# Two PSUM copies of the recurrent head group on one engine, in a one-layer hybrid decoder step

## The chip, the cores and the metric

The kernel runs on one core of a Trainium2 chip. The metric is the device time of one execution in microseconds; the median of several runs is compared. One execution was also taken by the hardware profiler, and all rows quoted here are from it.

## The reference

One layer of a decoder for 256 new prompt tokens and 8 single decode tokens: a half-step SwiGLU FFN, a mixer in which 16 attention heads (sliding window of 128, four key/value heads) stand beside 16 RWKV-7 heads, a second half-step FFN, and a final RMSNorm. What the change touches is the recurrence of the RWKV-7 heads:

```python
def wkv_scan(S0, r, logw, k, v, kk, a):
    def step(S, inp):
        r_t, lw_t, k_t, v_t, kk_t, a_t = inp
        sa = jnp.einsum('bhij,bhj->bhi', S, -kk_t)
        S = (S * jnp.exp(lw_t)[:, :, None, :] + sa[..., None] * (kk_t * a_t)[:, :, None, :]
             + v_t[..., None] * k_t[:, :, None, :])
        return S, jnp.einsum('bhij,bhj->bhi', S, r_t)
```

and the layer around it:

```python
def trunk_layer(x, attend, shift0, wkv0, lp):
    x = x + FFN_RES * swiglu(rmsnorm(x, n1), f1g, f1u, f1d)
    proj = rmsnorm(x, nm) @ w_in
    o_att, k_buf, v_buf = attend(q, k, v, sinks)
    o_rwkv, shift, S = rwkv_time_mix(proj[..., ATT_COLS:], shift0, wkv0, ...)
    x = x + jnp.concatenate([o_att, o_rwkv], axis=-1) @ w_out
    x = x + FFN_RES * swiglu(rmsnorm(x, n2), f2g, f2u, f2d)
```

The model width is 2048, the FFN width 5504, a head is 64 wide. All values are float32.

## The kernel before

All 264 tokens are columns of one activation tile of 128 x 264 per 128 features. Each weight chunk of 128 x 512 is loaded by SyncE (`raw`), rounded by ScalarE to `hi` (L127), and the rest `lo` = `raw` - `hi` is made by VectorE or GpSimd (L128, through the helper at L58). A gemm step multiplies `hi` and `lo` with the two parts of the activations, three matmuls for each 128 rows (`mm`, L74). Four buffers each of `hi` and `lo` and six of `raw` are in flight. Three PSUM banks (`acc`) serve the gemms, five (`m`, given out by `mp()`) everything else.

The execution goes through the first FFN, the mixer's input projection (`win`; its weights are loaded from 753.6 to 1088.4 us), the mixer's output projection (`wout`, loaded from 1089.8 to 1222.3 us), and the second FFN. The recurrence is not run token by token: the 256 prompt tokens are cut into four chunks of 64, and within a chunk the recurrence is solved with small triangular matrices. The work of the 16 RWKV heads is written as Python generators, which are advanced one step (`tick`) after each gemm step, so that their small instructions lie among the gemm's. `prep` treats a pair of heads, `chain` a batch of two pairs; there are four batches (`BATCH`), and the preps of the next batch stand among the steps of the chain before.

In `chain`, VectorE first inverts 32 x 32 blocks in 30 dependent steps (`st`, `Xt`, L573 and L574), through scratch in DRAM on both sides. Then come, in order:

- matmuls of the inverse `TT` with the chunk's keys (`pW`) and with its values (`pU`), L634. `pU` is one PSUM bank; the matmuls put the two heads of a pair into opposite halves of the partitions.
- L637: ScalarE copies `pW` to `W`. L638: VectorE copies one half of `pU` (64 x 512) into the tile `uv`. L639: ScalarE copies the other half into the same tile.
- matmuls `pP` (from `BT` and `W`) and `pG` (from `gm` and `W`), L647 and L650; ScalarE copies `pP` to `PT` (L653), VectorE adds `pG` to `KR` (L655).
- matmuls `pN` (L662) and `pY` (L668), which read `uv`; VectorE makes `N` from `pN` (L670).
- three steps over the chunks: `PT` and `KR` with the state, L679 and L683 (`m<-N,PT` in the profile), and VectorE's updates `Z` and `S`.

The copies of `prep` that lie beside these on ScalarE are those of the transposed keys (`kr`, L516) and of `BT` (L523, L525).

The order on each engine is not written out: a planner lays all instructions out on its own model of the engines' times, takes the earlier instruction of the program where several are ready, and gives out the buffers and PSUM banks in that order. Instructions under `high_priority` and `keep_in_program_order` are excepted. It sets all semaphores too, and keeps two accesses to one PSUM bank by different engines apart. On the chip each engine works through its list in order.

Of the kernel before, what the change touches and what calls it, by code (L numbers as in the profile page):

```python
# [24 lines left out]
HALF = (slice(0, 64), slice(64, 128))  # L25
# [22 lines left out]
def body(tc, I, O):  # L48
    nc = tc.nc
    V, A, G, TE, SP = nc.vector, nc.scalar, nc.gpsimd, nc.tensor, nc.sync  # L50
# [44 lines left out]
    with ExitStack() as ctx:  # L95
# [17 lines left out]
        def mp():  # L113
            return pp.tile([P, 512], F32, tag="m", bufs=NM, name=uid("m"))
# [243 lines left out]
        def mixing_body(mx, n2, n3, XD):  # L358
# [3 lines left out]
            def ring(shape, tag, bufs):  # L362
                return mx.tile(list(shape), F32, tag=tag, bufs=bufs, name=uid(tag))
# [186 lines left out]
            def chain(bt):  # L550
# [18 lines left out]
                for s in range(1, 31):  # L569
                    m, w = -(-s // ng), 31 - s  # L570
                    t = ring((ng * nr, m, w), "st", 2)
# [24 lines left out]
                def quads(k):  # L596
                    return slice(k * 4, k * 4 + 4), slice(k * P, k * P + P)
# [9 lines left out]
                for k in range(n):  # L607
                    c, x = quads(k)
# [9 lines left out]
                for k in range(n):  # L618
                    c, x = quads(k)
# [4 lines left out]
                uv = bt.UV  # L624
                W, PT = ring((P, n, 3, 64), "W", 1), ring((P, n, 3, 64), "PT", 1)
                N = ring((P, n, 4, 64), "N", 1)
                pW, pU = mp(), mp()
# [7 lines left out]
                                       bt.KR[k][HALF[h], a, c, :])  # L635
                pW, pU = (ps.rearrange("p (k c t) -> p k c t", k=n, c=4) for ps in (pW, pU))
                A.copy(W, pW[:, :, 1:4, :])  # L637
                V.tensor_copy(uv[HALF[0], :, :, HALF[0]].rearrange("p c k t -> p k c t"), pU[HALF[1]])  # L638
                A.copy(uv[HALF[1], :, :, HALF[1]].rearrange("p c k t -> p k c t"), pU[HALF[0]])  # L639
                yield  # L640
                pP, pG = mp(), mp()
                for k in range(n):
# [62 lines left out]
                for k in range(n):  # L705
                    p, o = bt.p0 + k, Ys[k]
# [169 lines left out]
            for kind, i in SEQ:  # L876
                if kind == "b":
                    bt = newbatch(i)
                    for k in range(BATCH[i]):
                        p = bt.p0 + k  # L880
                        x = [shifted(2 + 3 * p + j, tmp()) for j in range(3)]
                        spawn(prep(p, bt, k, *x))
                    bat.append(spawn(chain(bt)))
                    bts.append(bt)
                    if len(bat) == len(BATCH):
                        A.dma_start(O["sh"], shc)
                elif kind == "kv":
                    w, p = i // 2, i % 2
# [6 lines left out]
                else:  # L895
# [6 lines left out]
                    if i % 4 == 3:  # L902
                        p = i // 4
# [188 lines left out]
```

## Time and profile before

| | |
|---|---|
| median of 3 runs | 2003.16 us (2001.62 to 2003.61) |
| the profiled execution | 2001.57 us, span 1999.8 us |
| mean granted TensorE clock | 0.997 |
| TensorE matmuls | busy 1969.5 us, 17212 instructions |
| VectorE | busy 1301.4 us, 2546 instructions |
| ScalarE | busy 1065.4 us, 2137 instructions |
| GpSimd | busy 343.1 us, 437 instructions |
| L638, VectorE | 4 copies of 64 x 512, 0.69 us each |
| L639, ScalarE | 4 copies of 64 x 512, 0.58 us each |

PE is TensorE's matmuls, PEld its weight loads, DVE VectorE, ACT ScalarE, POOL GpSimd, SP SyncE. In a row of the timeline stand the start and the duration in us, the engine, the line, the operation with its output and inputs, and in brackets how long the engine was idle before it and who released it. Pool tiles are named by their tag: `m` is one of the five small PSUM banks, `acc` one of the three of the gemms.

### The profile page before, as it was taken

How to read it: one execution, taken by the hardware profiler on the slowest of the kernel's cores; microseconds unless marked ns; L12 is line 12 of the kernel's file. 1: busy time of each engine (PE TensorE's matmuls, PEld its weight loads, DVE VectorE, ACT ScalarE, POOL GpSimd, SP SyncE). 2: the span in 40 equal slices, each digit the busy share in tenths (PEclk: the TensorE clock that was granted, in tenths of full speed). 3: DMA queues.
4: the chain of work that ended last, by engine and by line, in shares of the span. 5: the costliest groups of instructions: out<-in, count | busy, mean ns of one | idle time of the engine just before them, and what ended most of it. 6: DMA issues, size and time to landing. Idle time of an engine off the chain costs nothing.

```text
span 1999.8 us, 45897 instructions
## 1 busy us (share of the span) xinstructions
PE 1969.5 (98%) x17212; PEld 1933.6 (97%) x17212; DVE 1301.4 (65%) x2546; ACT 1065.4 (53%) x2137; POOL 343.1 (17%) x437
## 2 busy tenths in 40 slices
PE   9999999999999999998998999999999999999998
PEld 9999999999999999997987899999999999999997
DVE  5865555655556577687867676765666666666665
ACT  5644444444444456775666765654444444444445
POOL 0401001010010121121124553120101001010012
PEclk9999999999999999999999999999999999999999
DMA  7666666655556667554555546565666666666654
GB/s 230 178 190 194 185 192 191 184 184 176 187 178 184 181 196 222 160 148 121 155 144 148 162 144 196 174 181 178 187 190 192 181 190 194 184 192 183 195 179 146
DMA packets 229232, 358.77 MB, mean 179 GB/s; under 512 B 42616, under 2 KB 84240, under 8 KB 229008
## 3 DMA queue, kind: packets, MB, share of 16 engines
q1 hardware_dynamic: 223120, 349.72, 57.9%
q10 hardware_dynamic: 5888, 6.11, 1.0%
q8 instruction: 135, 2.21, 0.4%
q14 instruction: 89, 0.73, 0.1%
HBM read 347.59 MB, written 10.22 MB: 179 GB/s over the span
## 4 chain that ended last, share of the span: by engine, by line
PE 91%; DVE 4%; DMA 2%; ACT 1%; issue 1%; SPq 1%; POOL 0%; ACTq 0%; DVEq 0%; POOLq 0%
PE acc L74 84%; PE m L74 6%; DVE lo L58 1%; DMA raw<-in_gu 1%; DVE st L58 1%; DVE Xt L58 1%; DMA raw<-in_win 0%; ACT t L68 0%; ACT hi L127 0%; DMA sb<-Xt 0%; DMA TT<-sb 0%; DVE y L58 0%; SPq L562 0%; DMA Xt<-sa 0%; SPq L563 0%
## 5 line engine op out<-in xcount | busy, mean ns | idle before, releaser
L127 ACT CAST hi<-raw 128x512 fp32r<-128x512 f32 (+2 forms) x1304 | 778.5, 601 | 818.0 <-PE acc L74 725.1
L58 DVE TENSOR_TENSOR lo<-raw,hi 128x512 fp32r<-128x512 f32 (+1 forms) x1248 | 854.4, 688 | 535.8 <-ACT hi L127 512.0
L74 PE MATMUL acc<-s,hi 128*128 128x264 f32 x5940 | 1111.7, 286 | 1.1 <-ACT hi L127 1.1
L74 PEld LDWEIGHTS acc<-s,hi 128*128 128x128 f32 x5940 | 923.3, 188 | 8.4 <-ACT hi L127 1.8
L74 PE MATMUL acc<-s,lo 128*128 128x264 f32 x2970 | 848.2, 286 | 4.9 <-DVE lo L58 4.6
L74 PEld LDWEIGHTS acc<-s,lo 128*128 128x128 f32 x2970 | 558.4, 188 | 9.5 <-DVE lo L58 6.4
L74 PE MATMUL acc<-t,hi 128*128 128x264 f32 x2752 | 502.8, 284 | 0.0
L74 PEld LDWEIGHTS acc<-t,hi 128*128 128x128 f32 x2752 | 425.9, 188 | 0.0
L74 PE MATMUL acc<-t,lo 128*128 128x264 f32 x1376 | 388.5, 284 | 0.0
L58 POOL TENSOR_TENSOR t<-t,t 128x264 f32<-128x264 f32 (+1 forms) x148 | 150.8, 1019 | 1148.6 <-ACT hi L127 789.9
L74 PEld LDWEIGHTS acc<-t,lo 128*128 128x128 f32 x1376 | 258.1, 188 | 0.1
L74 PE MATMUL acc<-y,hi 128*128 128x264 f32 x648 | 123.9, 284 | 0.0
L74 PEld LDWEIGHTS acc<-y,hi 128*128 128x128 f32 x648 | 101.2, 188 | 0.2
L74 PE MATMUL acc<-y,lo 128*128 128x264 f32 x324 | 91.3, 282 | 0.0
L58 DVE TENSOR_TENSOR t<-acc,t 128x264 f32<-128x264 f32 x156 | 67.4, 432 | 35.9 <-PE acc L74 35.7
L58 POOL TENSOR_TENSOR lo<-raw,hi 128x512 fp32r<-128x512 f32 x56 | 75.4, 1347 | 63.3 <-ACT hi L127 36.9
L58 POOL TENSOR_TENSOR o<-o,o 128x264 f32<-128x264 f32 x43 | 36.5, 848 | 187.4 <-ACT o L68 181.7
L74 PE MATMUL acc<-o,hi 128*128 128x264 f32 x324 | 62.4, 282 | 0.0
L74 PEld LDWEIGHTS acc<-y,lo 128*128 128x128 f32 x324 | 60.9, 188 | 0.0
L61 DVE SCALAR_TENSOR_TENSOR s<-acc,s 128x264 f32<-128x264 f32 x96 | 40.6, 428 | 15.9 <-PE acc L74 15.5
L74 PEld LDWEIGHTS acc<-o,hi 128*128 128x128 f32 x324 | 50.0, 188 | 0.0
L74 PE MATMUL m<-s,hi 128*128 128x264 f32 x260 | 48.1, 285 | 0.0
(252 smaller groups left out, 1336.9 us busy)
## 6 DMA issues: line engine op xcount, KB each, us to landing
raw<-in_gu SPq DMA_DIRECT2D x688, 256.0 KB, 3.4
raw<-in_dn SPq DMA_DIRECT2D x224, 256.0 KB, 2.9
raw<-in_win SPq DMA_DIRECT2D x152, 256.0 KB, 3.5
raw<-in_dn SPq DMA_DIRECT2D x160, 192.0 KB, 2.7
raw<-in_wout SPq DMA_DIRECT2D x48, 256.0 KB, 3.3
raw<-in_wout SPq DMA_DIRECT2D x32, 128.0 KB, 3.1
s<-xsp SPq DMA_DIRECT2D x16, 132.0 KB, 3.9
ld<-in_sT SPq DMA_DIRECT2D x16, 128.0 KB, 3.6
```

Of the source, the lines that this page charges most:

```text
L58: return e.tensor_tensor(out=out, in0=a, in1=b, op=op)
L61: return V.scalar_tensor_tensor(out=out, in0=a, scalar=s, in1=b, op0=op0, op1=op1)
L74: TE.matmul(out, lhsT, rhs, start=start, stop=stop, **k)
L127: A.copy(hi[:, :w], raw[:, :w])
```

## The change

Both halves of `pU` are copied into `uv` by ScalarE, in a loop over the two halves, the former VectorE half first. Nothing else is edited; the planner lays out the whole program anew.

```diff
                 A.copy(W, pW[:, :, 1:4, :])
-                V.tensor_copy(uv[HALF[0], :, :, HALF[0]].rearrange("p c k t -> p k c t"), pU[HALF[1]])
-                A.copy(uv[HALF[1], :, :, HALF[1]].rearrange("p c k t -> p k c t"), pU[HALF[0]])
+                for h in range(2):
+                    A.copy(uv[HALF[h], :, :, HALF[h]].rearrange("p c k t -> p k c t"), pU[HALF[1 - h]])
                 yield
```

## The prediction

> **What bounds the kernel now.** I read the page's engine line and chain first, then the rows of the two lines that the diff touches, then the stretches around their four executions.
>
> ```profile
> PE 1969.5 (98%) x17212; PEld 1933.6 (97%) x17212; DVE 1301.4 (65%) x2546; ACT 1065.4 (53%) x2137; POOL 343.1 (17%) x437
> PE 91%; DVE 4%; DMA 2%; ACT 1%; issue 1%; SPq 1%; POOL 0%; ACTq 0%; DVEq 0%; POOLq 0%
> ...
> L638 DVE COPY uv<-m x4: 692/694/694, 924.3 to 1134.1; 64x512 f32<-64x512 f32 x4
> L639 ACT COPY uv<-m x4: 577/578/579, 925.0 to 1135.5; 64x512 f32<-64x512 f32 x4
>   PEld m L74: 2.4, 2
>   PE m L74: 2.2, 2
> ```
>
> TensorE is busy for 98% of the span, so an edit on other engines is worth only what it takes out of TensorE's few waits, or out of stretches in which TensorE's clock is low. The diff touches four pairs of copies, one for each batch of heads, at 924, 996, 1055 and 1134 us. The last two lines are the waits of weight loads and matmuls for L639: TensorE stood 2.2 us for it, in two places. The windows show the first one as the odd one out (the last two rows are of batch 2):
>
> ```profile
> 924.00:925.00 1.00, 0.00 (x0) 0.00 (x0) 0.95 (x3) 0.01 (x1) 0.00 (x0) 0.65 0.18 68
> 925.00:931.00 6.00, 5.38 (x101) 5.14 (x102) 5.49 (x25) 3.09 (x8) 0.10 (x1) 0.50 0.18 44
> 931.00:932.00 1.00, 1.00 (x9) 1.00 (x9) 0.42 (x3) 0.62 (x2) 0.21 (x2) 0.93 0.06 16
> ...
> 1052.00:1056.00 4.00, 1.76 (x55) 1.34 (x53) 3.83 (x15) 3.17 (x9) 3.61 (x3) 1.00 0.61 181
> 1058.00:1063.00 5.00, 2.65 (x36) 2.33 (x33) 4.69 (x19) 0.62 (x1) 1.65 (x3) 1.00 0.66 209
> ```
>
> Columns: stretch and length, busy us of PE, PEld, DVE, ACT, POOL, then the granted clock, DMA share, GB/s. Around batch 0 the clock falls to 0.50 for over 6 us; VectorE is nearly full (5.49 of 6.00), ScalarE half empty.
>
> **Batch 0, step by step.** ScalarE's, VectorE's and TensorE's rows (start, duration, idle before and its releaser in brackets):
>
> ```profile
> 921.59 0.48 ACT L637 COPY W<-m 128x384 f32<-128x384 f32 x1
> 921.96 1.08 ACT L516 COPY kr<-m 64x128 f32<-64x128 f32 x4
> 923.06 0.37 ACT L523 COPY BT<-m 128x256 f32<-128x256 f32 x1
> 923.45 0.37 ACT L525 COPY BT<-m 64x256 f32<-64x256 f32 x1
> 924.99 0.58 ACT L639 COPY uv<-m 64x512 f32<-64x512 f32 x1 [1.18 <-DVE uv L638]
> 925.47 0.36 ACT L525 COPY BT<-m 64x256 f32<-64x256 f32 x1
> ...
> 924.02 0.22 DVE L58 TENSOR_TENSOR st<-X,Xt 128x55 f32<-128x55 f32 x1
> 924.26 0.69 DVE L638 COPY uv<-m 64x512 f32<-64x512 f32 x1
> 924.88 0.20 DVE L58 TENSOR_TENSOR Xt<-Xt,st 128x55 f32<-128x55 f32 x1
> 929.78 0.68 DVE L58 TENSOR_TENSOR N<-m,wc 128x512 f32<-128x512 f32 x1
> ...
> 917.12 1.15 PE L74 MATMUL m<-kr,TT 64*64 64x64 f32 x56
> 922.12 0.45 PE L74 MATMUL m<-uv,gm 64*64 64x64 f32 x8 [1.13 <-ACT W L637]
> 923.09 0.56 PE L74 MATMUL m<-BT,W 64*64 64x64 f32 x12
> 925.62 0.59 PE L74 MATMUL m<-gm,W 64*64 64x64 f32 x6 [1.97 <-ACT uv L639]
> 930.71 0.57 PE L74 MATMUL acc<-s,hi 128*128 128x264 f32 x1
> 932.43 0.27 PE L74 MATMUL m<-N,PT 64*64 64x64 f32 x2
> ```
>
> The matmuls that fill pU end at 917.12 + 1.15 = 918.27. VectorE's copy starts only at 924.26, 6 us later, without an idle gap: it stands in VectorE's queue behind the next batch's `st`/`Xt` steps. ScalarE's copy starts at 924.99, 0.04 after it ends; it reads the other half of the same PSUM bank and writes the same tile, and is kept behind. `gm,W` at 925.62 starts 0.05 after ScalarE's copy ends (925.57): it does not read uv, it takes over a PSUM bank (five in the ring), and this is pU's.
>
> *Removed*: four VectorE copies, and the handover between the engines. *Added*: four ScalarE copies of the 0.58 us form; on ScalarE the next instruction starts 0.48 after one (924.99 to 925.47). The pair then needs 0.48 + 0.58 = 1.06 us on one engine and waits for ScalarE alone. Both inputs are there at 918.27, so ScalarE can run them right behind W: at 921.96, done at 923.02 instead of 925.57. The kr copies (1.08 us) then end at about 924.00, and `gm,W` goes when both banks (pU's and that of the kr copies) are free: at about 924.05. Should the kr copies come first, the pair ends at 924.10, which is the same. TensorE ends `BT,W` at 923.65, so of its 1.97 us about 0.4 are left.
>
> The clock is the second term. The same stretch, `gm,W` to the next gemm, in batch 1:
>
> ```profile
> 997.60 0.39 PE L74 MATMUL m<-gm,W 64*64 64x64 f32 x6
> 1000.46 0.39 PE L74 MATMUL acc<-s,hi 128*128 128x264 f32 x1
> 1002.85 0.27 PE L74 MATMUL m<-N,PT 64*64 64x64 f32 x2 [0.79 <-DVE st L58]
> ...
> 996.24 0.69 DVE L638 COPY uv<-m 64x512 f32<-64x512 f32 x1
> 996.85 0.21 DVE L58 TENSOR_TENSOR Xt<-Xt,st 128x60 f32<-128x60 f32 x1
> 996.97 0.58 ACT L639 COPY uv<-m 64x512 f32<-64x512 f32 x1 [0.94 <-DVE uv L638]
> ...
> 1054.69 0.27 PE L74 MATMUL m<-BT,W 64*64 64x64 f32 x2 [2.12 <-ACT W L637]
> 1055.45 0.58 ACT L639 COPY uv<-m 64x512 f32<-64x512 f32 x1 [0.81 <-DVE uv L638]
> 1056.08 1.09 PE L74 MATMUL m<-uv,BT 128*64 128x64 f32 x29 [0.20 <-ACT uv L639]
> 1062.06 0.27 PE L74 MATMUL m<-N,PT 64*64 64x64 f32 x2 [2.35 <-DVE st L58]
> ...
> 1135.50 0.58 ACT L639 COPY uv<-m 64x512 f32<-64x512 f32 x1
> 1137.80 1.15 PE L74 MATMUL m<-uv,BT 128*64 128x64 f32 x32
> ```
>
> Batch 1 takes 1000.46 - 997.60 = 2.86 us, batch 0 takes 930.71 - 925.62 = 5.09: the low clock costs 2.23 there. With the stall it makes 4.2 us, the most that batch 0 can give. What is late next is N: TensorE's `N,PT` needs it, and VectorE, full, makes it at 929.78. One copy fewer moves it up by 924.88 - 924.26 = 0.62, to an end at 929.84; `N,PT` then starts near 929.9 instead of 932.43, which is 2.5 us, the least if VectorE keeps its order. N's own matmuls would be done some 3 us sooner, though, and the planner may put N ahead of some of the 0.2 us steps. I take the middle, 3.4.
>
> Here a rule of the Trainium skill speaks against the term (TensorE: Matmul & The Clock Gate, HAM oscillation — how this bites in real kernels): TensorE should only avoid idle gaps above some 3.4 us. By it the drop should not be there, and the batch would give the stall alone. The trace differs: the clock fell within the second of two gaps, 1.13 and 1.97 us. It does not follow from the gaps alone either, since gaps of 2.12 and 2.35 us in batch 2 left the clock at 1.00. So the drop may come and go from run to run; that goes into the range.
>
> **Batches 1 to 3.** In batch 1 no matmul waits for the pair, since 997.60 is just behind its end at 997.55; but `N,PT` waits 0.79 for VectorE's queue, which loses one copy: 0.6 us (996.85 - 996.24). In batch 2 the 0.20 us at 1056.08 goes and comes back at `N,PT`, which waits 2.35 for VectorE: 0.6 in all. ScalarE's extra 0.48 us lies in its idle 1.18, 0.94 and 0.81 us. In batch 3 ScalarE has no idle gap; its pair would end 0.5 later than 1136.08, and the first use is at 1137.80, so 1.7 us of gemm cover it: nothing. Without those covers it would be 0.48 each, 1.9 in all.
>
> **Sum**: 3.4 + 0.6 + 0.6 = 4.6 us, between 2.5 + 0 + 0 and 4.2 + 1.2 = 5.4. The profiled execution took 2001.57 us (span 1999.8 and 1.8 around it), so it would be 1997.0. The three timed runs have their median at 2003.16, 1.6 above it; against that, 1998.6. About 0.2% (4.0 us) is what a measurement of this kernel can tell from no change.
>
> **The rivals.**
>
> *The wait moves, slower.* ScalarE works in order, and the planner lays out all engines anew around its own clock. The pair ahead of the kr and BT copies holds these back by 0.96 us in batches 0 and 1, and with them the PSUM banks that they empty, of which there are five. If the planner sees less cover there than the chip needs, one group of small matmuls stands before a held bank, as `gm,W` does now. The nearest price is the longest wait of this stage, 2.35, and the low clock behind it, 2.23: 4.6 us a place. If batch 0 keeps its 4.2 us loss as well and one place is added, the result is 4.6 above the median, 2007.8; two places make 2012. It decides from about 2 us of new wait on. For it: W alone holds TensorE for 1.13 and 2.12 us already. Against it: in batch 1 TensorE goes past the pair without a wait, and in batch 0 the new wait for the kr copies comes to 0.4.
>
> *The pair is planned late, no change.* If both copies stand behind the BT copies, where L639 stands now, they run from 923.82 to 924.88; TensorE still waits 1.25 us, the clock may still fall, and the gain is 0.7 + 1.2 = 1.9: 2001.3.
>
> *The two halves ran side by side.* The Trainium skill (PSUM — Partial Sum Buffer, PSUM bank collisions raise a hardware error) says that two engines may use different quadrants of one bank at the same time, and the two halves are different quadrants. Were the halves side by side, the pair took the longer copy, 0.69, and on ScalarE alone takes 1.06: 4 x 0.37 = 1.5 us lost, 2004.7. The trace shows the second waiting for the first in three batches (1.18, 0.94, 0.81), so this has next to no weight.
>
> *A better plan.* If the new order also removes the two waits for W, 1.13 and 2.12 us, the gain is 4.6 + 3.2 = 7.8: 1995.4.
>
> **How the numbers follow.** The forecast's case has 0.52: the stall has a clear cause that the edit removes, but the new order is not in the trace. Of it 0.35 lies over 4.0 us of gain and 0.17 under. The late pair has 0.08, the side-by-side reading 0.01, the better plan 0.05, the moved wait 0.34, of which 0.02 within 4.0 us. Faster: 0.35 + 0.05 = 0.40. Within: 0.17 + 0.08 + 0.01 + 0.02 = 0.28. Slower: 0.32. The range goes from the better plan's 1995.4, rounded to 1995.0, to one added wait, 2007.8; the forecast's own range is 1997.8 to 2000.7.
>
> **What would show it.** Right: in batch 0 ScalarE's two uv copies within a microsecond of W; no 1.97 us wait of `gm,W`, at most 0.5; a granted clock of 1.00 through 925 to 931; `N,PT` 2 to 4 us earlier against the gemms around it. Wrong: a new TensorE wait of over 2 us for kr, BT or W copies; the low clock in another place of the stage 900 to 1150 us; or the time won there lost again at a later wait for VectorE's `lo` or for the `Xt` chain.

## The result: slower by 3 us, and the profile after

The changed kernel takes 2005.72 us (median of 21 runs, 2003.37 to 2010.84); the kernel before, run beside it, 2002.45 (21 runs, 2000.05 to 2004.81). The ratio is 1.0016, 95% interval 1.0010 to 1.0023: slower by 2 to 4.6 us, about 3.2. The forecast was a gain of 4.6 us. The profiled execution took 2005.03 us (span 2003.2) against 2001.57 (1999.8).

The page's engine line after:

```profile
PE 1971.7 (98%) x17212; PEld 1937.0 (97%) x17212; DVE 1300.0 (65%) x2542; ACT 1067.9 (53%) x2141; POOL 339.7 (17%) x437
```

The copies' row after, with who waited for them (us, times):

```profile
L639 ACT COPY uv<-m x8: 577/580/587, 922.4 to 1138.5; 64x512 f32<-64x512 f32 x8
...
  PEld m L74: 0.2, 1
```

Stretches after, with the columns of the prediction (PE, PEld, DVE, ACT, POOL, granted clock, DMA share, GB/s):

```profile
924.00:925.00 1.00, 0.35 (x18) 0.28 (x18) 0.86 (x5) 0.95 (x4) 0.00 (x0) 1.00 0.29 104
925.00:931.00 6.00, 4.35 (x118) 3.96 (x114) 5.55 (x24) 5.07 (x12) 0.10 (x1) 1.00 0.24 58
...
1034.00:1037.00 3.00, 3.00 (x17) 2.97 (x16) 0.85 (x2) 0.52 (x2) 0.00 (x0) 0.54 0.53 134
1064.00:1068.00 4.00, 2.78 (x25) 2.69 (x26) 3.76 (x18) 0.62 (x1) 0.00 (x0) 0.62 0.49 191
908.00:911.00 3.00, 3.00 (x14) 3.00 (x15) 3.00 (x9) 2.16 (x7) 1.58 (x3) 0.50 0.39 114
```

TensorE does as many matmuls as before and VectorE has four instructions fewer. TensorE's wait for the second copy, 2.2 us before, is gone, and 0.2 us of a weight load is left. The clock around batch 0 is 1.00. It is low elsewhere instead: near 909, 1035 and 1066 us. The first of these is not the change's doing: up to 922 us the list of every engine is that of before. Yet the execution after is already 1.2 us behind there, so not all of the 3.4 us between the two profiled executions is of the change.

Batch 0 in the timeline after (start, duration, engine, line, idle before and its releaser):

```profile
921.90 0.48 ACT L637 COPY W<-m 128x384 f32<-128x384 f32 x1
922.40 1.17 ACT L639 COPY uv<-m 64x512 f32<-64x512 f32 x2
923.60 1.07 ACT L516 COPY kr<-m 64x128 f32<-64x128 f32 x4
...
930.08 0.68 DVE L58 TENSOR_TENSOR N<-m,wc 128x512 f32<-128x512 f32 x1
...
918.32 1.15 PE L74 MATMUL m<-kr,TT 64*64 64x64 f32 x56
924.73 0.27 PE L74 MATMUL m<-gm,W 64*64 64x64 f32 x2 [0.65 <-ACT kr L516]
930.91 0.27 PE L74 MATMUL m<-N,PT 64*64 64x64 f32 x2 [1.41 <-DVE Xt L58]
```

This is what the prediction drew: the pair directly behind W, the wait of `gm,W` down from 1.97 to 0.65, and `N,PT` at 930.91. From the first `kr,TT` matmul of the batch (917.12 before, 918.32 after) to `N,PT` it was 15.31 us and is 12.59: 2.7 us won.

Where it was given back is seen 7 us later. The same rows after, then before:

```profile
937.83 0.43 DVE L591 STREAM_TRANSPOSE TN<-TT 32x256 f32<-32x256 f32 x1 [4.24 <-DMA TT<-sb]
938.52 0.44 DVE L61 SCALAR_TENSOR_TENSOR S<-m,wc,Z 128x64 f32<-128x64 f32 x2
938.83 0.27 PE L74 MATMUL m<-S,PT 64*64 64x64 f32 x2 [1.43 <-DVE S L61]
980.50 0.39 PE L74 MATMUL acc<-s,lo 128*128 128x264 f32 x1 [2.14 <-DVE lo L58]
1014.86 0.43 DVE L591 STREAM_TRANSPOSE TN<-TT 32x256 f32<-32x256 f32 x1 [3.33 <-DMA TT<-sb]
1015.80 0.46 DVE L61 SCALAR_TENSOR_TENSOR S<-m,wc,Z 128x64 f32<-128x64 f32 x2
1016.40 0.68 PE L74 MATMUL m<-y,C 128*128 128x264 f32 x2 [1.12 <-DVE S L61]
1025.20 0.71 PE L74 MATMUL m<-sgl,ld 128*128 128x264 f32 x2 [1.68 <-ACT t L68]
1065.22 0.37 PE L74 MATMUL m<-N,PT 64*64 64x64 f32 x2 [3.40 <-DVE Xt L58]
```

```profile
936.28 0.47 DVE L61 SCALAR_TENSOR_TENSOR S<-m,wc,Z 128x64 f32<-128x64 f32 x2
939.27 0.43 DVE L591 STREAM_TRANSPOSE TN<-TT 32x256 f32<-32x256 f32 x1 [2.52 <-DMA TT<-sb]
980.25 0.39 PE L74 MATMUL acc<-s,lo 128*128 128x264 f32 x1 [0.85 <-DVE lo L58]
1011.28 0.47 DVE L61 SCALAR_TENSOR_TENSOR S<-m,wc,Z 128x64 f32<-128x64 f32 x2
1015.72 0.43 DVE L591 STREAM_TRANSPOSE TN<-TT 32x256 f32<-32x256 f32 x1 [2.26 <-DMA TT<-sb]
1022.89 0.71 PE L74 MATMUL m<-sgl,ld 128*128 128x264 f32 x2 [1.68 <-ACT t L68]
```

`TN` (L591) is VectorE's transpose of the next batch's inverse `TT`, which has just come back through DRAM; its result is read only by a `TN,gm` matmul at 987.71, some 50 us later. But VectorE works in order, and while the first of the two stands waiting for its DMA, all else on VectorE stands behind it. In the kernel before, `S` came ahead of `TN` (936.28, 1011.28). In the newly planned order `TN` is ahead of `S` in batches 0 and 1, the state update sits out a wait of 4.24 and 3.33 us, and TensorE with it: new waits of 1.43 and 1.12 us. The wait for `lo` near 980 grew from 0.85 to 2.14. Summed over all TensorE's waits between 933 and 1033 us, 5.2 us before became 9.2 after. From the first `kr,TT` matmul of batch 0 to the `kr,bk` matmuls near 1030, a stretch of the same work in both, it was 112.7 us (917.12 to 1029.83) and is 113.8 (918.32 to 1032.15): the 2.7 us are gone, and 1.1 more.

Two causes thus stand against each other: theory A, the new order costs more than the copies win; rival B, the copies themselves cost (longer holds of PSUM banks, ScalarE fuller). The experiments separate them. The clock is no third one: one minus the granted clock, times the span, comes to 9.6 us on average in the 21 runs after and to 9.2 in the 84 runs of the kernel before beside the experiments (8.8 to 9.5 by group), too little for 3.2.

### The profile page after: what moved, and what is told of

Same layout as the page of the kernel before. It is cut to its first block, busy times and chain, and to the rows that moved or that the text cites. A ratio compares the mean times of both kernels' runs of the same rounds, so it can differ in the third digit from the quotient of the medians.

```text
span 2003.2 us, 45905 instructions
## 1 busy us (share of the span) xinstructions
PE 1971.7 (98%) x17212; PEld 1937.0 (97%) x17212; DVE 1300.0 (65%) x2542; ACT 1067.9 (53%) x2141; POOL 339.7 (17%) x437
## 4 chain that ended last, share of the span: by engine, by line
PE 91%; DVE 4%; DMA 2%; ACT 1%; issue 1%; SPq 1%; POOL 0%; ACTq 0%; DVEq 0%; POOLq 0%
PE acc L74 84%; PE m L74 6%; DVE lo L58 1%; DVE st L58 1%; DVE Xt L58 1%; DMA raw<-in_gu 1%; DMA raw<-in_win 1%; ACT hi L127 0%; DMA sb<-Xt 0%; DVE y L58 0%; SPq L563 0%; ACT L68 0%; ACT t L68 0%; SPq L562 0%; DVE t L723 0%
```

## The experiments

All ratios are against the kernel before, run on the same chip, with 95% intervals; its medians were 2003.70, 2004.26 and 2002.78 us in the three groups (e1 to e4, e5 to e8, e9 to e12).

**Holding an order.** To change the copies without a new plan, the lists of all five engines are written out and held: edges without a semaphore tie every instruction to the one ahead of it on its engine. No run holds before's lists with nothing moved; but in the trace of e1 the matmuls from 50 to 922 us start within 0.12 us of before's, so the holding itself costs nothing that shows there.

```diff
-        body(tc, I, O)
+        body(tc, I, O); pin(tc, nc)
+def pin(tc, nc):
+    ins = {i.name: i for i in nc.cur_bb.bb.instructions}
+    info = mybir.DependencyInfo(mybir.DependencyClass.NoSync, mybir.DependencyReason.DATA)
+    for part in ORDER:            # one list of instruction numbers for each engine
+        last = None
+        for i in (ins[f"I-{n}"] for n in part):
+            if last is not None:
+                tc.add_manual_dep(i, last.name, info, reason="pin")
+            last = i
```

**e1: the copies changed, the order as before.** The changed code, with before's lists, in which only the four pairs move:

```diff
 ScalarE: ... W,
+             uv half 0, uv half 1,      (batches 0 to 3; shown: 0 and 1)
              kr, kr, kr, kr, BT, BT,
-             uv half 1, ...
 VectorE: ... st,
-             uv half 0,
              Xt, ...
```

> All four pairs of copies on ScalarE, right behind W, but every engine's list otherwise held in the order of the kernel before, instruction by instruction (scheduling edges; TensorE's, GpSimd's and SyncE's lists are the same, VectorE's lacks four copies). Theory A, the loss lies in the new order that the planner made: here the time goes down by 2.5 to 5 us against before, the wait of gm,W in batch 0 (1.97 us) is gone and the clock stays at 1.00 there. Rival B, the loss lies in the copies themselves (four more instructions of 0.58 us in ScalarE's list): the time goes up by 2 to 4 us, and a wait of TensorE for ScalarE appears in a batch.

2001.96 us (11 runs), ratio 0.9990 (0.9981 to 0.9999): 2 us faster, where the change as planned is 3.2 slower. The copies do win, less than expected, and the clock did not stay at 1.00: it falls for 3.4 us from 924.0. Its rows in batch 0:

```profile
922.13 1.17 ACT L639 COPY uv<-m 64x512 f32<-64x512 f32 x2
924.46 0.59 PE L74 MATMUL m<-gm,W 64*64 64x64 f32 x6 [0.54 <-ACT kr L516]
929.11 0.68 DVE L58 TENSOR_TENSOR N<-m,wc 128x512 f32<-128x512 f32 x1
930.16 0.27 PE L74 MATMUL m<-N,PT 64*64 64x64 f32 x2
938.67 0.43 DVE L591 STREAM_TRANSPOSE TN<-TT 32x256 f32<-32x256 f32 x1 [4.19 <-DMA TT<-sb]
942.13 0.69 PE L74 MATMUL m<-y,C 128*128 128x264 f32 x2 [0.85 <-DVE S L61]
```

`TN` starts at 938.67 where it was at 939.27: what batch 0 wins ahead of it only lengthens the wait for the DMA (2.52 to 4.19), and 0.60 us comes through, about the one copy that VectorE's list has lost. From `kr,TT` (917.15) to `kr,bk` (1028.28) e1 takes 111.1 us, 1.6 less than before.

**e2: the order of after, the copies as before** (the original two lines, each copy at its old neighbours).

```diff
-                for h in range(2):
-                    A.copy(uv[HALF[h], :, :, HALF[h]]..., pU[HALF[1 - h]])
+                V.tensor_copy(uv[HALF[0], :, :, HALF[0]]..., pU[HALF[1]])
+                A.copy(uv[HALF[1], :, :, HALF[1]]..., pU[HALF[0]])
+    ORDER: the changed kernel's lists
```

> The reverse: one half is copied by VectorE, the other by ScalarE as before, each behind the same instruction as in the kernel before, but every engine's list otherwise held in the order of the changed kernel. Theory A: slower than before by 3 to 8 us, that is the new order's loss without the copies' gain. Rival B: within 1.5 us of before.

2005.72 us (11 runs), ratio 1.0016 (1.0007 to 1.0025). Without the change, its order alone costs what the change costs. So in the new order the copies win nothing that can be told (e2 and after have the same ratio, their difference known to about 2 us), and e1's 2 us can't simply be added. `gm,W` waits for the copies again (1.87), and the order's own waits are there as after:

```profile
924.77 0.27 PE L74 MATMUL m<-gm,W 64*64 64x64 f32 x2 [1.87 <-ACT uv L639]
938.14 0.27 PE L74 MATMUL m<-S,PT 64*64 64x64 f32 x2 [0.96 <-DVE S L61]
979.16 0.39 PE L74 MATMUL acc<-s,lo 128*128 128x264 f32 x1 [1.42 <-DVE lo L58]
1064.82 0.27 PE L74 MATMUL m<-N,PT 64*64 64x64 f32 x2 [3.39 <-DVE Xt L58]
```

**e3: only batch 0 changed, old order.**

```diff
-                V.tensor_copy(uv[HALF[0], ...
+                (A.copy if bt.i == 0 else V.tensor_copy)(uv[HALF[0], ...
+    ORDER: before's lists, batch 0's pair moved as in e1
```

> As the first, but only batch 0 has both copies on ScalarE; the old order is held, so batches 1 to 3 are as in the kernel before. By the prediction's working batch 0 gives 2.5 to 4.2 us of the whole gain; theory A expects a gain of 2 to 4 us, and no less than 1 us less than all four batches give. Rival B: within 1 us of before, since only one added copy is left.

2003.02 us (11 runs), 0.9994 (0.9985 to 1.0003): not told apart from no change, and not from e1. The 2 to 4 us expected for batch 0 did not come; from `kr,TT` to `kr,bk` it takes 111.6 us, 1.1 less than before.

**e4: both on ScalarE, late** (old order, the first copy put where the second stood, behind the BT copies).

```diff
 ScalarE: ... W, kr, kr, kr, kr, BT, BT,
+             uv half 0,
              uv half 1, ...
```

> All four pairs on ScalarE with the old order held, but each pair at the place of the ScalarE half before, in batches 0 and 1 behind the kr copies and two of the BT copies. By the prediction's rival of the late pair: TensorE still waits about 1.25 us in batch 0, and the gain is 1 to 3 us, 1 to 2 us less than right behind W. If it gains as much as right behind W, the place does not matter; if it loses, ScalarE's list is the limit (rival B).

2002.24 us (11 runs), 0.9997 (0.9988 to 1.0005): no difference that can be told, less than the 1 to 3 us expected, where the place behind W gives 0.9990. The intervals of e1 and e4 overlap, so the place is not shown to matter. The wait of `gm,W` is 1.29, near the 1.25 of the prediction's late pair.

**e5: the order of after, two places mended.** In VectorE's list the `S` updates go ahead of `TN` in batches 0 and 1, and two `lo` ahead of the first inversion step near 976 us.

```diff
 VectorE (batches 0 and 1):
+             S, S,
              TN, ...
-             S, S, ...
 VectorE (near 976 us):
+             lo, pj, lo,
              st, Xt, st, ... RECIPROCAL,
-             lo, pj, lo, ...
```

> The changed kernel with its own order held on every engine, and three things moved in VectorE's list alone, to where the kernel before has them: in batch 0 the second pair of S updates and in batch 1 the last pair stand ahead of the transposes TN, which wait for a DMA, and near 975 us two lo and one pj stand ahead of the first st of the third inversion, which waits for a DMA too. Theory A', the loss is TensorE's work queued behind VectorE's waits for DMA: 1.5 to 3.5 us faster than the changed kernel, that is -2 to +2 us against before; TensorE's waits at S,PT (1.43 us, near 938) and y,C (1.12 us, near 1016) are gone and the one for lo near 980 is under 1 us. If the loss lies elsewhere in the new order (TensorE's or ScalarE's list), the time stays at 3 to 4 us over before.

2006.22 us (11 runs), 1.0013 (1.0004 to 1.0022): not mended. The waits of `S,PT` (1.43) and of batch 1's `y,C` (1.12) did go, but TensorE then waits for the steps behind `TN` instead: 1.11 at 942 us, where after had none. The moved `lo` now waits for ScalarE's cast (2.73 us idle at 976.47), and the wait near 980 stays:

```profile
981.23 0.39 PE L74 MATMUL acc<-s,lo 128*128 128x264 f32 x1 [1.88 <-DVE lo L58]
1064.40 0.27 PE L74 MATMUL m<-N,PT 64*64 64x64 f32 x2 [3.39 <-DVE Xt L58]
```

So it is not enough that `S` stands ahead of `TN`; whatever stands behind `TN` is held.

**e6 and e7: `TN` out of the way, old order.** The six `TN` transposes of batches 1 to 3 move down VectorE's list, behind vector work of the preps that needs no DMA (at 946, 1016 and 1082 us): e6 with the changed copies as in e1, e7 with the copies as before.

```diff
 VectorE (three places):
-             TN, ... TN,
              S, lo, t, bk, ...
+             TN, TN,
```

> The old order held, all four pairs of copies on ScalarE right behind W, and the six transposes TN of batches 1 to 3 moved down VectorE's list by a few instructions, so that nothing that TensorE needs soon stands behind their wait for a DMA. Theory A': what batch 0 gains (2.3 us at N,PT) is not cut to 0.6 us at TN any more; 2 to 4 us less than with the old order and TN in its old place, so 4 to 6 us less than before. If the gain stays at about 2 us, another wait of the same length stands behind TN.

> The old order held and the copies as in the kernel before (one half on VectorE), only the six transposes TN moved down as in the run beside it. It says what TN's place is worth by itself. Theory A': 1 to 3 us less than before, and less than with the copies on ScalarE as well; if it gives as much as both together, the copies add nothing.

e6: 1995.26 us (5 runs), 0.9964 (0.9951 to 0.9976), the best version, 7 us faster than before. e7: 1997.67 us (8 runs), 0.9972 (0.9962 to 0.9983). The intervals overlap, so the copies' own share on top (2.4 us by the medians, 1.6 by the ratios) is not shown by this pair alone; it agrees with e1's 2. Both won more than expected (by the ratios 7.2 us against 4 to 6, and 5.6 against 1 to 3). From `kr,TT` to `kr,bk` the traces read 106.5 us in e6 and 108.2 in e7, against 112.7 before and 111.1 in e1, one execution of each; `TN`'s place is thus worth some 4.5 us with either copies, and the copies some 1.6 with either place. VectorE's idle time ahead of `TN` for the DMA (us, times), in the kernel before:

```profile
  DMA TT<-sb: 10.3, 5
```

in the kernel after:

```profile
  DMA TT<-sb: 13.6, 6
```

and in e6:

```profile
  DMA TT<-sb: 2.2, 1
```

TensorE's waits in e6 between 933 and 1033 us, 2.7 us in all:

```profile
950.60 0.71 PE L74 MATMUL m<-sgl,ld 128*128 128x264 f32 x2 [0.70 <-ACT t L68]
978.64 0.39 PE L74 MATMUL acc<-s,lo 128*128 128x264 f32 x1 [0.89 <-DVE lo L58]
1000.85 0.27 PE L74 MATMUL m<-N,PT 64*64 64x64 f32 x2 [0.59 <-DVE st L58]
1025.51 1.71 PE L74 MATMUL m<-kr,bk 64*128 64x128 f32 x16 [0.48 <-DVE y L61]
```

The 1.68 us for ScalarE's `t` near 1022, in both kernels, is gone too: `t` is fed by the VectorE steps that stood behind `TN`.

**e8: the two lines exchanged, no engine changed, planned anew.**

```diff
-                V.tensor_copy(uv[HALF[0], :, :, HALF[0]]..., pU[HALF[1]])
                 A.copy(uv[HALF[1], :, :, HALF[1]]..., pU[HALF[0]])
+                V.tensor_copy(uv[HALF[0], :, :, HALF[0]]..., pU[HALF[1]])
```

> No engine changes: the two copies stand in the other order in the program (ScalarE's half first, VectorE's second), and the planner lays everything out anew. The work is that of the kernel before; 1372 lines of TensorE's list differ from it. Theory A (the new layout decides): a difference from before of either sign, 1 to 6 us. Rival B (the copies' work decides): within 1 us of before.

2009.97 us (5 runs), 1.0033 (1.0021 to 1.0046). An edit that moves no work between engines costs 6.6 us, twice the change itself. ScalarE's half now goes first; but TensorE's two waits for the copies are 1.62 and 0.70 us where they were 1.97 and 0.20, so that isn't where 6.6 us come from. Over the whole execution TensorE's waits come to 24.6 us, 20.6 before; the longest new ones are at 1118 (1.77) and 1145 us (1.12), where the trace before has none. This is what a new plan can do.

**e9: the order of after, `TN` late.** The move of e6 in the changed kernel's lists.

> The changed kernel's order on every engine, but in VectorE's list the six TN transposes of batches 1 to 3 stand where they stood in the run of late TN with the old order. Theory 1, the new order loses only because it puts the TN transposes ahead of S: all of the difference goes, 7 to 9 us below before, as with the old order. Theory 2, the order loses in other places too: the same 5.5 to 7 us are won as with the old order, but from 3.2 us above before, so 2.5 to 4 us below before.

1997.61 us (11 runs), 0.9976 (0.9967 to 0.9985): 4.8 us below before, 8 below the same order with `TN` early. That is more than the move wins in the old order (0.9964 against e1's 0.9990, 5.2 us): the result lies between the two expectations, nearer to the second. By the ratios the new order loses 5.2 us with `TN` early (after against e1) and 2.4 with `TN` late (e9 against e6), each known to about 2 us: `TN` is about half of the loss. Its remaining waits from 933 to 1060 us:

```profile
977.44 0.39 PE L74 MATMUL acc<-s,lo 128*128 128x264 f32 x1 [2.15 <-DVE lo L58]
1000.64 0.27 PE L74 MATMUL m<-N,PT 64*64 64x64 f32 x2 [0.52 <-DVE st L58]
1025.30 1.55 PE L74 MATMUL m<-kr,bk 64*128 64x128 f32 x16 [0.91 <-DVE y L61]
1056.78 0.27 PE L74 MATMUL m<-N,PT 64*64 64x64 f32 x2 [3.39 <-DVE Xt L58]
```

Against e6 two of these are longer, `lo` by 1.26 and `kr,bk` by 0.43. `N,PT` in batch 2 is longer by 1.0 too (3.39 against 2.37), but e6 waits 1.34 for W there and e9 does not. So 1.7 us of waits are left to the new order, and 2.4 us in the ratios, whose intervals overlap. But its wait for W in batch 0 is 0.27 where e6 has 1.13, and from `kr,TT` to `kr,bk` it needs 106.7 us, e6 106.5 (after 113.8, e1 111.1): up to 1030 us nearly all that the new order loses is `TN`'s place, by one execution of each.

**e10, e11, e12: half old, half new.** All with the changed copies; the lists are joined where batch 1's (or 2's) `pW` and `pU` matmuls begin.

```diff
+    e10:  before 993 us the old lists (as e1), behind it the changed kernel's
+    e11:  before 993 us the changed kernel's lists, behind it the old ones
+    e12:  before 1050 us the old lists, behind it the changed kernel's
```

> All four pairs on ScalarE. Every engine keeps the old order up to batch 1's pW and pU matmuls (about 993 us) and has the changed kernel's order from there. Theory 1, the new order loses in batch 0's stretch (TN ahead of S, the wait for lo near 980): 1 to 2 us below before, like the run with the old order throughout. Theory 2, it loses in batch 1's stretch, 993 to 1053 us, where the trace after is 2.6 us longer than with the old order: 1 to 3 us above before.

> The reverse: the changed kernel's order up to batch 1's pW and pU matmuls, the old order from there. Theory 1 (the loss is in batch 0's stretch): 2 to 4 us above before. Theory 2 (it is in batch 1's stretch): 1 us below before to 0.5 above.

> The old order up to batch 2's pW and pU matmuls (about 1050 us), the changed kernel's order from there (123 places of TensorE's list differ from the old order). Theories 1 and 2: like the old order throughout, 1 to 3 us below before, since the last stretch is 1.2 us shorter in the trace after. Theory 3, the loss is behind 1050 us, where N,PT waits 3.4 us in place of 2.4: 1 us above before or more.

| | old order until | ratio (95%) |
|---|---|---|
| e1 | the end | 0.9990 (0.9981 to 0.9999) |
| e12 | 1050 us | 0.9995 (0.9986 to 1.0003) |
| e10 | 993 us | 1.0009 (1.0000 to 1.0018) |
| after | nowhere | 1.0016 (1.0010 to 1.0023) |
| e11 | new until 993 us, then old | 1.0000 (0.9991 to 1.0008) |

The loss builds up in steps: 1.0 us by the order behind 1050 us, 2.8 between 993 and 1050, 1.4 ahead of 993 (2.0 by e11 against e1). Each step is known to about 2 us, so only the whole (5.2) and the gap between e10 and e1 (3.8) are clear of the noise. The middle one reads largest, as theory 2 had it (e10 above before, e11 at it), but is not shown to be. e12 lies at the near edge of its 1 to 3 us: 1.0 by the ratio, 0.3 by the medians.

## Why the prediction was wrong

**Right: the stall of batch 0, and its clock in this execution.** The pair stands behind W, `gm,W` waits 0.65 (forecast 0.4, at most 0.5), the clock is 1.00 through 925 to 931, and 2.7 us are won to `N,PT`, between the bounds of 2.5 and 4.2 and under the 3.4 taken. That the clock stayed up was in part luck: in e1 the pair stands at the same place, and the clock fell. One price was off a little: the pair takes 1.17 us (922.40 to 923.57), not 1.06. The 0.48 in it was read from a copy followed by one out of another bank; whether that is the reason was not tested.

**Wrong: "N is late next" was taken as the end of batch 0's working.** The step put 3.4 us into the sum by holding that what is won at `N,PT` is won at the end. In e1, where nothing but the copies differs, `N` is 0.67 earlier (929.11), TensorE passes `N,PT` without a wait and 2.3 us earlier (930.16, 932.43 before), and 0.60 is left when VectorE reaches `TN`, whose DMA wait takes the rest. The row that said so was in the trace before: 2.52 us idle at 939.27. e6, e7 and e9 show what the waits at `TN` cost the stage: with the six moved, 5 to 8 us go.

**Wrong: that the order around the copies stays.** This step turned the sign. The sum, 3.4 + 0.6 + 0.6, was worked out in the old lists, and even there e1 gives 2.0 and not 4.6. The planner draws new lists; with the changed copies they cost 5.2 us against the old ones (after against e1), and without them 3.2 (e2 against before). The working allowed for a new order only within batch 0 (N ahead of some 0.2 us steps) and as a rival.

**The rival of the other sign had the right cause and the wrong mechanism.** It had the planner put work where the cover is too short, but saw it in PSUM banks held by the kr and BT copies; that wait is 0.65. The real one, for about half of the loss by the ratios of e9, is a transfer's wait inside VectorE's list. Of the signs of a miss that the prediction named, two appeared: the low clock in other places of the stage, and time lost again at later waits for `lo` (0.85 to 2.14) and for the `Xt` chain (2.35 to 3.40). The first says little: e1, which is faster, has drops near 1031 and 1062 too.

**Batches 1 to 3.** Batch 1's `N,PT` wait fell by 0.28 of its 0.79, not 0.6 (by 0.12 in e1), and batch 2's 2.35 is 2.37 in e1. The "better plan" did come: TensorE's waits for W are 0.25 in batch 0 (1.13 before) and none in batch 2 (2.12), and uv's 0.20 is gone as well. But in batch 2 `N,PT` then waits 3.40 in place of 2.35, and the rest goes at `TN` and `lo`. In batch 3 nothing waits for the pair, as forecast.

**The clock term, 2.23, was no fixed cost.** In e1 and e12 the lists are the same up to 1050 us, and so are TensorE's waits there (1.15, 0.19 and 0.54 against 1.13, 0.19 and 0.54). The stretch reads in e1

```profile
924.00:931.00 7.00, 6.54 (x131) 6.14 (x132) 6.38 (x30) 5.66 (x13) 0.32 (x3) 0.76 0.16 47
```

and in e12

```profile
924.00:931.00 7.00, 6.32 (x109) 5.94 (x110) 6.15 (x27) 5.39 (x12) 0.32 (x3) 1.00 0.17 44
```

One order, one execution of each, and only in one did the clock fall. So a drop seen in one trace is a chance of a cost; the range had that, the sum did not. And the cost is less than the working took: from `kr,TT` to `N,PT` e1 needs 13.01 us with its 3.4 us of low clock, e12 12.76 with none, since in e12 `N,PT` waits 0.68 for VectorE instead. The 2.23 were read at the next gemm, ahead of that wait. The stall may still feed the drops: in the runs that hold the old order, one minus the clock, times the span, averages 6.7 us in e1, 6.0 in e3 and 6.8 in e6, but 8.7 in e4 and 8.0 in e7, where `gm,W` still waits, and 8.8 in the kernel before beside e1; single executions vary by 2 to 3 us.

**Open.** Why the planner put `TN` ahead of `S` was not traced to its costs. What the new order loses apart from `TN` (about 2 us by the ratios of e9 and e6, if it is more than noise) has no place yet: e9's waits at `lo` near 980 and at `kr,bk` are longer, but the stretch up to `kr,bk` is not. The run that moved the `lo` (e5) did not remove its wait, `kr,bk` was not tried alone, and nothing was tried behind 1050 us but the order as a whole (e12).

## What to carry to other kernels

Where a planner orders the program, an edit of two lines is an edit of the whole order: price it as "the copies' own gain plus a draw of a new order", and split the two by holding the order. When a trace shows an in-order engine idle for a transfer whose result is needed much later, that row is the first thing to mend: whatever is won ahead of it ends there. Here moving six transposes was worth 5 to 8 us, the copies about 2 in the old order and nothing that can be told in the new one.

## What the runs showed of the hardware

The granted clock falls to 0.50 for about 3.4 or 6.8 us at a time: summed over 840 to 1200 us of each trace, one minus the clock comes to 3.4, 5.1, 6.8 or 8.6 us. What such a drop costs depends on what it meets. The one at 924 in e1 cost 0.25 us (13.01 against 12.76 above). The one near 1031 in e1, among gemm matmuls, cost 1.6: the same matmul lies 2.0 us later than in e12 at 1022 and 3.6 later at 1040. Over the 222 executions whose clock is on record, executions of one kernel differ by 0.33 us of time (standard error 0.05) for each us of one minus the clock, times the span. The drops come mostly near the same places (908, 925, 1031, 1057 to 1066 us) in some executions and not in others, behind waits of 1.2 us and less as well: in e1 the longest wait shortly before the drop at 924 is 1.15 us. The Trainium skill (TensorE: Matmul & The Clock Gate, HAM oscillation — how this bites in real kernels) puts the rule at idle gaps above some 3.4 us; the same page (A second HAM failure mode: psum-queue depth-cycling) tells of a clock that oscillates from many short idle times, and that is nearer to what these runs show.
